# Moving low-part products to the end of ten weight tiles, one add to GpSimd, three exponentials behind the squares and one transpose a step up, in a hybrid decoder layer

## The chip, the core and the metric

The kernel runs on one core of a Trainium2 chip. The core has TensorE (PE: matrix products; its weight loads are listed as PEld), VectorE (DVE), ScalarE (ACT), GpSimd (POOL) and SyncE (SP); each takes its own instructions in order. ACT, SP and POOL also issue DMA transfers. The metric is the device time of one execution in microseconds (us), the median of three runs: 831.07 us before the change (829.67 to 834.61).

## What is computed

The reference is one layer on 512 tokens of 1024 channels, all in float32:

```
u = rmsnorm(h);  proj = u @ w_in      # GLU pairs, q, k, v, r, low-rank gate, gate A, gate B
c = a * sigmoid(g);  c = causal_depthwise_conv(c, width 31)
y_conv = silu(layernorm(c)) @ w_conv_out
gk = log_sigmoid(g_low @ w_gate_up + b_gate) / 16
o = chunked_gla(q, k, v, gk)          # 4 heads, chunks of 64 tokens
o = o * rsqrt(mean(o*o) + EPS) * gla_norm_g * silu(r)
y_gla = o @ w_gla_out
h = h + (sigmoid(gate_a) * y_conv + sigmoid(gate_b) * y_gla) @ w_o
u2 = rmsnorm(h);  z = causal_depthwise_conv(u2 @ w_ffn_up, width 3)
h = h + (silu(z_a) * z_b) @ w_ffn_down
return rmsnorm(h)
```

Inside a head the decays come from gk: b is the running sum of gk within a chunk of 64 tokens, and exp(b), exp(-b) and exp(b_last - b) scale q and k.

## The kernel before, in words

**Products in two parts.** Each float32 operand is split into a high part, rounded to the type fp32r, and a low part, the rest. A product is then three matmuls into one PSUM bank: low weight with high activation, high with low, and high with high. `mm3` issues these three (L395, L396, L397). A column tile (`col_tile`) holds 128 output channels over 512 tokens: eight k-steps of `mm3`, 24 matmuls, into one of five banks "mm". The result has channels on partitions. A second set of three banks is called "ax".

**Weights.** SP loads a tile of 128 x 1024 into `raw` (four buffers). `split_weight` makes `whi` (four buffers) by an ACT cast (L342; L323 for tiles that are handled in other ways). The low part `wlo` (four buffers) is made in one of two ways. Usually DVE subtracts (L351, L324). For tiles in the table `ADDED`, ACT writes the negated, rounded raw tile into `wlo` (L344), and POOL issues a DMA that adds the same weights from DRAM to it (L345), so that what remains is the rest; the low part is ready when that transfer has landed. A `wlo` buffer is written anew when the last matmul that reads it is through. `ADDED` holds, among others, five tiles of `w_glu` (4, 6, 8, 12 and 14), all eight of `w_qk`, and all of `w_gb` and `w_gla`.

**What sets the order.** The program is written in Python against a tile framework with a scheduler. It places each engine's instructions from the order in which the code stands, the data they need and the free buffers. Some stretches are pinned to the order written. `with tc.issue_after(x)` puts the instructions of the block that run on x's engine behind x there; other engines are not bound. The 31 convolution taps of each channel tile (L813, on DVE; the first one on ACT, L810) stand in lists, `chains`, from which a share is placed whenever a weight tile is taken, so DVE works at them beside the matmuls.

**The stages, by the times of the profile.** First normalisation and first v and r products (to about 32 us), GLU, r and v with the seven-product scheme for 2x2 blocks (to about 160), four heads (160 to 302), `w_gla`, `w_ga` and `w_conv` with the layer norm of the convolution (to about 435), `w_o` and the second norm (to about 490), then feed-forward.

**The heads.** The loop over h is staggered. In turn h it issues, for the new head h, `decays` (DVE: scan L1065, difference L1071, small copies L1075 to L1077; ACT: exponentials L1067, L1068, L1072), `queries` and `keys`; and for the old head h-1 `scores`, `states`, `outputs` and `gated`, with further weight tiles between them (`between`). `outputs` makes o in two pairs of token tiles: PE products (L1137, L1139), ACT squares with a running sum (L1142, twice for each pair), DVE adds EPS (L1144), POOL raises to the power -1/2 (`rsqrt`, L443), DVE multiplies by the root and the gate (L1150, twice for each pair). `gated` transposes o on PE (L1156), eight transposes of 128 x 128. Between the last matmul of `outputs` and these transposes PE has one weight tile to work at.

**The second norm.** `seven` runs `w_o` in steps. The token tiles of the residual are complete at different steps: tiles 0 and 1 after the step s4, tiles 2 and 3 after the last step, a22. A complete tile gets squares on ACT (L1336), the sum on DVE (L1341), the root on POOL (L443), the scaling into `un` on ACT (L491), transposes on PE (L474), the gain on DVE (L483) and the split into high part `uh` (ACT, L485) and low part `ul` (DVE, L486). `o_at` is called after the matmuls of each half step and places `to_channels`, the turn of a tile. The feed-forward begins with four tiles of `w_up`, each first for tokens 0 to 255 and then for 256 to 511, in matmuls of 256 columns.

Of the kernel before, what the change touches and what calls it, by code (L numbers as in the profile page):

```python
# [10 lines left out]
F32 = mybir.dt.float32  # L11
# [6 lines left out]
P = 128  # L18
# [27 lines left out]
UP_SEVEN = (6, 7, 10, 11, 14, 15, 18)  # L46
UP_BESIDE = (1, 3, 4, 5, 9, 20, 13, 16, 17)
ADDED |= {("w_up", j) for i in UP_BESIDE for j in (i, FT + i)}
SEVEN = {"w_o": KT // 2, "w_down": FT // 2, "w_r": KT // 2, "w_v": KT // 2}


# [27 lines left out]
def trunk_layer(ctx: ExitStack, tc: tile.TileContext, a: dict, out: bass.AP):  # L79
# [65 lines left out]
    gate_up = cp.tile([P, HEADS * DK], F32R, name="gate_up")  # L145
    ones = cp.tile([P, P], F32, name="ones")
    mhalf = cp.tile([P, NT], F32, name="mhalf")
    shares = cp.tile([P, P], F32, name="shares")
    run64 = cp.tile([P, T], BF16, name="run64")
    keep = cp.tile([P, P], U8, name="keep")  # L150
# [2 lines left out]
    def load_consts():  # L153
        tc.keep_in_program_order(nc.sync.dma_start(pp, a["pp"]))
        nc.gpsimd.memset(shares, -1.0 / D)
        nc.gpsimd.memset(run64, 1.0)
        nc.gpsimd.memset(run64[:, 0:T:64], 0.0)

        kf = tmp(P)
        nc.gpsimd.memset(kf, 1.0)  # L160
        nc.gpsimd.affine_select(
            kf, kf, pattern=[[1, P]], compare_op=ALU.is_ge, fill=0.0, base=0, channel_multiplier=-1
        )
        nc.gpsimd.tensor_copy(keep, kf)
        nc.gpsimd.memset(att, 0.0)
# [139 lines left out]
    def split_weight(between=None):  # L305
        if len(ready) < len(order):
            while len(raws) <= len(ready):
                load()
            raw = raws[len(ready)]
            name, spec = order[len(ready)]  # L310
            if name in SEVEN or name == "w_up7":
                raw = operand(name, raw, *spec) if name in SEVEN else up_operand(raw, *spec)
                n = raw.shape[-1]
                if name == "w_up7" and spec[1] == "m":
                    both = wp.tile([P, D], F32R, tag="raw", name=nm("wm"), bufs=4)
                    nc.scalar.copy(both[:, :T], raw)
                    nc.vector.tensor_tensor(both[:, T:], raw, both[:, :T].bitcast(F32), ALU.subtract)
                    ready.append((both[:, :T], both[:, T:]))
                    load()
                    return  # L320
                hi = wp.tile([P, D], F32R, tag="whi", name=nm("whi"), bufs=4)[:, :n]
                lo = wp.tile([P, D], F32R, tag="wlo", name=nm("wlo"), bufs=4)[:, :n]
                nc.scalar.copy(hi, raw)  # L323
                pace[0] = nc.vector.tensor_tensor(lo, raw, hi.bitcast(F32), ALU.subtract)  # L324
                if name in SEVEN:
                    sum_on(name, *spec)
                skipped = name in INNER and raws[len(ready)] is None
                ready.append((hi, lo))
                if not skipped:
                    load()  # L330
                return
            hi = wp.tile([P, D], F32R, tag="whi", name=nm("whi"), bufs=4)
            if order[len(ready)][0] == "w_low":
                nc.scalar.copy(hi, raw)
                if order[len(ready)][1] == 0:
                    part_lo = lambda t: t.rearrange("p (k c) -> p k c", c=P)[:, :, :RANK]
                    nc.vector.tensor_tensor(part_lo(hi), part_lo(raw), part_lo(hi.bitcast(F32)), ALU.subtract)
                ready.append((hi, None))
                load()
                return  # L340
            lo = wp.tile([P, D], F32R, tag="wlo", name=nm("wlo"), bufs=4)
            nc.scalar.copy(hi, raw)  # L342
            if order[len(ready)] in ADDED:
                pace[0] = nc.scalar.activation(lo, raw, AF.Copy, scale=-1.0)  # L344
                nc.gpsimd.dma_start(lo, a[name][spec], accum_op=ALU.add)  # L345
                ready.append((hi, lo))
                load()
                return
            if between:
                between()  # L350
            pace[0] = nc.vector.tensor_tensor(lo, raw, hi.bitcast(F32), ALU.subtract)  # L351
            ready.append((hi, lo))
            load()
# [37 lines left out]
    def mm3(acc, l, r, first, last, more=False):  # L391
# [4 lines left out]
        nc.tensor.matmul(acc, lh, rl, start=False, stop=False, **kw)  # L396
        nc.tensor.matmul(acc, lh, rh, start=False, stop=last, **kw)  # L397

    def col_tile(w, acts, acc=None, lo=0, hi=T):

        if acc is None:
            acc = mm_bank()
        for k in range(KT):
            s = slice(k * P, (k + 1) * P)
            ah, al = acts[k]
            mm3(acc[:, lo:hi], (w[0][:, s], w[1][:, s]), (ah[:, lo:hi], al[:, lo:hi]), k == 0, k == KT - 1)
        return acc

    def row_half(name, j0, n, acts, nk, done, tok_inner, middle=None):
# [641 lines left out]
    class Head:  # L1051
# [77 lines left out]
        def outputs(self):  # L1129
            self.o = tp.tile([P, NT, DV], F32, tag="x", name=nm("o"), bufs=3)  # L1130
            for g in range(2):
                po = ax_bank()
                ss = small(2, "ss2")
                for i in range(2):
                    p = 2 * g + i
                    half = po[:, i * DV : (i + 1) * DV]
                    nc.tensor.matmul(half, att[:, p, :], self.v(p), start=True, stop=p == 0)  # L1137
                    if p:
                        nc.tensor.matmul(half, flat(self.q, p, 0), self.s[p], start=False, stop=True)  # L1139
                for i in range(2):  # L1140
                    half = po[:, i * DV : (i + 1) * DV]
                    nc.scalar.activation(junk(DV), half, AF.Square, scale=1.0 / 16.0, accum_out=ss[:, i : i + 1])  # L1142
                v = small(2, "var2")
                nc.vector.tensor_scalar(v, ss, EPS, None, ALU.add)  # L1144
                r = rsqrt(v, 2)
                for i in range(2):
                    t = 2 * g + i
                    gate = sr[t, self.h // 2][:, (self.h % 2) * DV : (self.h % 2 + 1) * DV]
                    half = po[:, i * DV : (i + 1) * DV]
                    nc.vector.scalar_tensor_tensor(self.o[:, t, :], half, r[:, i : i + 1], gate, ALU.mult, ALU.mult)  # L1150
# [22 lines left out]
    def between(h, i):  # L1173
# [4 lines left out]
        else:  # L1178
            gate_b(6 + i)

    heads = [Head(h) for h in range(HEADS)]
    for h in range(HEADS + 1):
        old = heads[h - 1] if h else None
        new = heads[h] if h < HEADS else None
        if new:
            new.decays()
            if h == 0:
                for y in sr.values():
                    behind(lambda: nc.scalar.activation(y, y, AF.Silu))
# [167 lines left out]
    def o_at(step, i):  # L1357
        if (step, i) == ("n3", 0):
            u2.extend(new_acts())
            first = tp.tile([P, D], F32, tag="gain", name=nm("f2"), bufs=1)  # L1360
            to_channels(normed[0], u2, 0, lambda g: first[:, g * T : (g + 1) * T])
        if (step, i) == ("a22", 0):
            to_channels(normed[1], u2, 1, lambda g: btmp())

    seven("w_o", O_PAIRS, mixed, o_complete, o_at)
# [220 lines left out]
    def by_parts(w):  # L1586

        acc = mm_bank()
        for k in range(KT):
            s = slice(k * P, (k + 1) * P)  # L1590
            mm3(acc, (w[0][:, s], w[1][:, s]), acts2[k], k == 0, k == KT - 1)
            yield acc

    for gi, pairs in enumerate(GROUPS):
        acts = []
# [123 lines left out]
```

## Time and profile before

| what | value |
| --- | --- |
| median of three runs | 831.07 us (829.67 to 834.61) |
| the profiled execution, its own time | 828.47 us |
| its span, first to last instruction | 826.8 us |
| PE busy | 813.3 us, 98% of the span |
| DVE busy | 676.8 us, 82% |
| ACT busy | 471.0 us, 57% |
| POOL busy | 123.1 us, 15% |
| granted TensorE clock | 0.998 |

Busy time of PE is modelled: matmuls overlap, so that a matmul row of 0.39 us is followed by the next after about 0.23 us. What PE loses at a place is therefore read from the distances of the start times rather than from the idle column. A row of the timeline gives start, duration, engine, line, operation, what it writes and reads with shapes, a count, and in brackets the idle time ahead of it and what ended it. A small loss on PE is the time of the kernel; idle time of another engine is none.

### The profile page before, as it was taken

The numbers are of one execution on the slowest core, as the hardware profiler recorded it, in microseconds if no ns is written. First come the engines' busy times: TensorE is split into PE (matmuls) and PEld (weight loads), VectorE is DVE, ScalarE is ACT, GpSimd is POOL, SyncE is SP. The second block draws the span as 40 slices with busy tenths as digits, with TensorE's granted clock in tenths as the row PEclk, the third lists the DMA queues.
The fourth block names the chain that finished last, engine by engine and source line by source line (L and its number), as shares of the span: only waits on it lengthen the run. The fifth ranks groups of instructions, "written<-read, shape, count | busy, mean of one in ns | idle before, by whom it ended". The sixth has DMA issues, their size and how long they took to land.

```text
span 826.8 us, 11023 instructions
## 1 busy us (share of the span) xinstructions
PE 813.3 (98%) x4090; PEld 689.9 (83%) x4090; DVE 676.8 (82%) x991; ACT 471.0 (57%) x669; POOL 123.1 (15%) x144
## 2 busy tenths in 40 slices
PE   8999999999999999999999999999999999999996
PEld 7988878878888888888888898888788888988885
DVE  6898978999989889854689768789858888588896
ACT  7664546695443553359344659655446543667554
POOL 2021101311122121000001012111112111220111
PEclk9999999999999999999999999999999999999999
DMA  9999849558666578221447539356835647557562
GB/s 324 310 327 222 209 116 230 129 160 211 150 131 154 134 195 202 77 102 51 153 92 205 183 116 237 93 146 153 217 93 149 166 89 217 153 153 202 131 128 101
DMA packets 50213, 136.65 MB, mean 165 GB/s; under 512 B 4624, under 2 KB 17184, under 8 KB 50160
## 3 DMA queue, kind: packets, MB, share of 16 engines
q1 hardware_dynamic: 37456, 90.91, 31.2%
q0 software_dynamic: 12528, 44.83, 30.5%
q8 instruction: 32, 0.52, 0.3%
q10 hardware_dynamic: 176, 0.20, 0.1%
q14 instruction: 21, 0.17, 0.1%
HBM read 133.84 MB, written 6.29 MB: 169 GB/s over the span
## 4 chain that ended last, share of the span: by engine, by line
PE 78%; DVE 11%; DMA 4%; issue 3%; ACT 2%; POOL 1%; SPq 0%; POOLq 0%; ACTq 0%; DVEq 0%
PE mm L396 22%; PE mm L395 22%; PE mm L397 22%; DVE c L813 4%; PE ax L395 2%; DMA wlo<-in_w_glu_dram 2%; PE mm L663 2%; PE ax L396 2%; PE ax L397 2%; DVE wlo L324 1%; DMA kept<-rows 1%; DMA x<-in_x_dram 1%; PE ax L1137 1%; DVE tmp L1378 1%; PE ax L474 0%
## 5 line engine op out<-in xcount | busy, mean ns | idle before, releaser
L395 PE MATMUL mm<-uh,wlo 128*128 128x512 f32 (+1 forms) x636 | 237.5, 374 | 3.5 <-DMA wlo<-in_w_glu_dram 1.9
L396 PE MATMUL mm<-ul,whi 128*128 128x512 f32 (+1 forms) x636 | 234.9, 369 | 0.2 <-DVE ul L486 0.2
L397 PE MATMUL mm<-uh,whi 128*128 128x512 f32 (+1 forms) x636 | 234.5, 369 | 0.0
L813 DVE SCALAR_TENSOR_TENSOR c<-h,pp,c 128x507 f32<-128x507 f32 (+20 forms) x240 | 169.9, 733 | 2.8
L395 PEld LDWEIGHTS mm<-uh,wlo 128*128 128x128 f32 x636 | 119.9, 189 | 22.9 <-DMA wlo<-in_w_glu_dram 2.1
L397 PEld LDWEIGHTS mm<-uh,whi 128*128 128x128 f32 x636 | 119.8, 188 | 20.5
L396 PEld LDWEIGHTS mm<-ul,whi 128*128 128x128 f32 x636 | 120.1, 189 | 18.7 <-DVE ul L486 0.7
L342 ACT CAST whi<-raw 128x1024 fp32r<-128x1024 f32 x94 | 97.4, 1042 | 36.7 <-PE mm L397 29.0
L344 ACT ACTIVATE wlo<-raw 128x1024 fp32r<-128x1024 f32 x47 | 49.5, 1058 | 69.6 <-PE mm L395 65.5
L323 ACT CAST whi<-raw 128x1024 fp32r<-128x1024 f32 (+1 forms) x53 | 54.0, 1027 | 52.6 <-PE mm L397 36.1
L324 DVE TENSOR_TENSOR wlo<-raw,whi 128x1024 fp32r<-128x1024 f32 (+1 forms) x53 | 65.8, 1249 | 11.5 <-ACT whi L323 11.0
L1378 DVE SCALAR_TENSOR_TENSOR tmp<-mm,pp,tmp 128x511 f32<-128x511 f32 (+1 forms) x88 | 64.5, 742 | 12.6 <-ACT tmp L1376 12.2
L351 DVE TENSOR_TENSOR wlo<-raw,whi 128x1024 fp32r<-128x1024 f32 x47 | 56.9, 1220 | 16.7 <-ACT whi L342 16.3
L323 ACT CAST whi<-kept 128x1024 fp32r<-128x1024 f32 (+1 forms) x44 | 44.3, 1009 | 37.7 <-PE mm L397 25.6
L324 DVE TENSOR_TENSOR wlo<-kept,whi 128x1024 fp32r<-128x1024 f32 (+1 forms) x44 | 52.3, 1196 | 4.3 <-ACT whi L323 4.1
L1376 ACT ACTIVATE tmp<-mm,pp 128x512 f32<-128x512 f32 x44 | 33.3, 775 | 11.6 <-PE mm L397 11.6
L1298 DVE TENSOR_TENSOR hres<-hres,mm 128x512 f32<-128x512 f32 (+1 forms) x49 | 32.4, 670 | 2.5 <-PE mm L397 2.3
L345 POOL DMA_DIRECT2D wlo<-in_w_up_dram x18 | 15.6, 866 | 95.5 <-ACT wlo L344 77.6
L396 PE MATMUL mm<-wlo,sh 128*128 128x512 f32 x66 | 25.9, 393 | 0.0
L397 PE MATMUL mm<-whi,sh 128*128 128x512 f32 x66 | 25.7, 390 | 0.0
L395 PE MATMUL mm<-h,wlo 128*128 128x512 f32 x64 | 25.4, 397 | 0.0
L395 PE MATMUL mm<-whi,sl 128*128 128x512 f32 x66 | 25.2, 391 | 0.2 <-ACT whi L323 0.2
(361 smaller groups left out, 1635.1 us busy)
## 6 DMA issues: line engine op xcount, KB each, us to landing
raw<-in_w_up_dram SPq DMA_DIRECT2D x44, 512.0 KB, 4.4
wlo<-in_w_up_dram POOLq DMA_DIRECT2D x18, 512.0 KB, 7.4
raw<-in_w_glu_dram SPq DMA_DIRECT2D x16, 512.0 KB, 5.9
raw<-in_w_down_dram SPq DMA_DIRECT2D x15, 512.0 KB, 5.1
kept<-in_w_down_dram POOLq DMA_DIRECT2D x10, 512.0 KB, 5.3
raw<-in_w_v_dram SPq DMA_DIRECT2D x8, 512.0 KB, 6.0
rows<-in_w_r_dram SPq DMA_DIRECT2D x16, 256.0 KB, 6.4
raw<-in_w_qk_dram SPq DMA_DIRECT2D x8, 512.0 KB, 5.1
```

Of the source, the lines that this page charges most:

```text
L323: nc.scalar.copy(hi, raw)
L324: pace[0] = nc.vector.tensor_tensor(lo, raw, hi.bitcast(F32), ALU.subtract)
L342: nc.scalar.copy(hi, raw)
L344: pace[0] = nc.scalar.activation(lo, raw, AF.Copy, scale=-1.0)
L351: pace[0] = nc.vector.tensor_tensor(lo, raw, hi.bitcast(F32), ALU.subtract)
L395: nc.tensor.matmul(acc, ll, rh, start=first, stop=False, **kw)
L396: nc.tensor.matmul(acc, lh, rl, start=False, stop=False, **kw)
L397: nc.tensor.matmul(acc, lh, rh, start=False, stop=last, **kw)
L813: nc.vector.scalar_tensor_tensor(y[:, s:], c[:, : T - s], w, y[:, s:], ALU.mult, ALU.add)
L1298: nc.vector.tensor_tensor(hres[t, n][:, c], hres[t, n][:, c], x[:, c], op)
L1376: nc.scalar.activation(z, acc, AF.Identity, bias=pp[:, PP_FB + m : PP_FB + m + 1], scale=w[2])
L1378: nc.vector.scalar_tensor_tensor(z[:, s:], acc[:, : T - s], w[j], z[:, s:], ALU.mult, ALU.add)
```

## The change

Five edits. `LOW_LAST_IN` names ten tiles of `ADDED` (`w_glu` 4 and 8, all `w_qk`). In these, `col_products` issues the 16 products with the high weight first and the eight with the low weight last; all other column tiles keep their order, and the number of matmuls is the same everywhere. In `outputs` EPS is added on GpSimd from a small constant tile instead of on VectorE. From the third head on, the ACT instructions of `decays` stand behind the last square of the head two before it. The second norm's turn of token tile 1 is placed at the step ("n3", 1) instead of ("a22", 0). `by_parts` yields as before, after every third product.

```
-                ready.append((hi, lo))
+                ready.append((hi, lo, (name, spec) in LOW_LAST_IN))

+LOW_LAST_IN = {("w_glu", 4), ("w_glu", 8)} | {("w_qk", m) for m in range(KT)}

+    eps = cp.tile([P, 2], F32, name="eps")
+        nc.gpsimd.memset(eps, EPS)

+    def col_products(w, acts, acc, lo=0, hi=T):
+
+        late = [(1, 0, k) for k in range(KT)] if w[2:] and w[2] else []
+        todo = [p for k in range(KT) for p in ([(0, 0, k), (0, 1, k)] if late else [(1, 0, k), (0, 1, k), (0, 0, k)])]
+        todo += late
+        for n, (low_w, low_a, k) in enumerate(todo):
+            l, r = w[low_w][:, k * P : (k + 1) * P], acts[k][low_a][:, lo:hi]
+            nc.tensor.matmul(acc[:, lo:hi], l, r, start=n == 0, stop=n == len(todo) - 1)
+            yield n
+
     def col_tile(w, acts, acc=None, lo=0, hi=T):
-
         if acc is None:
             acc = mm_bank()
-        for k in range(KT):
-            s = slice(k * P, (k + 1) * P)
-            ah, al = acts[k]
-            mm3(acc[:, lo:hi], (w[0][:, s], w[1][:, s]), (ah[:, lo:hi], al[:, lo:hi]), k == 0, k == KT - 1)
+        for _ in col_products(w, acts, acc, lo, hi):
+            pass
         return acc

-                    nc.scalar.activation(junk(DV), half, AF.Square, scale=1.0 / 16.0, accum_out=ss[:, i : i + 1])
+                    squared[0] = nc.scalar.activation(junk(DV), half, AF.Square, scale=1.0 / 16.0, accum_out=ss[:, i : i + 1])
                 v = small(2, "var2")
-                nc.vector.tensor_scalar(v, ss, EPS, None, ALU.add)
+                nc.gpsimd.tensor_tensor(v, ss, eps, ALU.add)

+    squared = [None]
     heads = [Head(h) for h in range(HEADS)]
     for h in range(HEADS + 1):
         old = heads[h - 1] if h else None
         new = heads[h] if h < HEADS else None
+        if squared[0] is None:
+            new.decays()
+        elif new:
+            with tc.issue_after(squared[0].ins):
+                new.decays()
         if new:
-            new.decays()

-        if (step, i) == ("a22", 0):
+        if (step, i) == ("n3", 1):
             to_channels(normed[1], u2, 1, lambda g: btmp())
```

How the rows move on the engines is seen at three places. In the names, `uh` and `ul` are the high and low parts of the activations (two tiles each, for channels 0 to 511 and 512 to 1023), `whi` and `wlo` those of a weight tile, `mm` and `ax` PSUM banks; numbers are buffers' numbers and differ between the two programs, as do line numbers.

PE, the end of tile 8 of `w_glu`, before (the last k-step, then the next matmuls of the v products):

```order
L395 MATMUL mm_1121<-uh_107,wlo_1069 128x512
L396 MATMUL mm_1121<-ul_108,whi_1068 128x512
L397 MATMUL mm_1121<-uh_107,whi_1068 128x512
L395 MATMUL mm_979<-whi_1075,ul_108 128x512
L396 MATMUL mm_979<-wlo_1076,uh_107 128x512
```

And PE at the end of the same tile now:

```order
L409 MATMUL mm_1123<-uh_108,whi_1070 128x512
L409 MATMUL mm_1123<-ul_109,whi_1070 128x512
L409 MATMUL mm_1123<-uh_106,wlo_1071 128x512 x4
L409 MATMUL mm_1123<-uh_108,wlo_1071 128x512 x4
L398 MATMUL mm_981<-whi_1077,ul_109 128x512
```

The eight products with `wlo` stand together at the end, so the tile's first read of `wlo` comes after 16 matmuls, and its last read two matmuls later than before.

ACT, around the squares of head 0 (`junk,ss` rows), before; `tmp<-b` are exponentials of the decays of heads 2 and 3, `tmp<-tmp` the third one of head 2, `c<-h` the first tap of a convolution:

```order
L344 ACTIVATE wlo_1932<-raw_1707 128x1024
L342 CAST whi_1931<-raw_1707 128x1024
L1068 ACTIVATE tmp_1989<-b_1986 128x512
L1072 ACTIVATE tmp_1990<-tmp_1990 128x512
L344 ACTIVATE wlo_2002<-raw_1759 128x1024
L342 CAST whi_2001<-raw_1759 128x1024
L1142 ACTIVATE junk_1905,ss_345_1901<-ax_1900 128x256
L810 ACTIVATE c_2008<-h_1146,pp 128x512
L1142 ACTIVATE junk_1907,ss_345_1901<-ax_1900 128x256
L1067 ACTIVATE tmp_2241<-b_2239 128x512
L1142 ACTIVATE junk_1921,ss_351_1916<-ax_1915 128x256
L1142 ACTIVATE junk_1923,ss_351_1916<-ax_1915 128x256
```

And ACT at the same place now:

```order
L347 ACTIVATE wlo_1934<-raw_1709 128x1024
L347 ACTIVATE wlo_2004<-raw_1761 128x1024
L345 CAST whi_2003<-raw_1761 128x1024
L1152 ACTIVATE junk_1907,ss_345_1903<-ax_1902 128x256
L820 ACTIVATE c_2010<-h_1148,pp 128x512
L1152 ACTIVATE junk_1909,ss_345_1903<-ax_1902 128x256
L1152 ACTIVATE junk_1923,ss_351_1918<-ax_1917 128x256
L1152 ACTIVATE junk_1925,ss_351_1918<-ax_1917 128x256
L1077 ACTIVATE tmp_1990<-b_1988 128x512
L1078 ACTIVATE tmp_1991<-b_1988 128x512
L1082 ACTIVATE tmp_1992<-tmp_1992 128x512
```

All three exponentials of head 2 now follow the fourth square of head 0, and the first one of head 3 no longer stands among the squares. On DVE, the difference (L1071) and the small copies of head 2 and the scan (L1065) of head 3 move with them, from ahead of head 0's o (L1150) to behind it.

PE in the last steps of `w_o`, before (products of the step n3 read `sums`, those of a22 read `h`; `un` is the scaled token tile 1):

```order
L395 MATMUL mm_3801<-whi_4025,h_3771 128x512
L396 MATMUL mm_3801<-wlo_4026,h_3770 128x512
L397 MATMUL mm_3801<-whi_4025,h_3770 128x512
L474 MATMUL ax_4108<-ident,un_4016 128x128 x4
L474 MATMUL ax_4109<-ident,un_4016 128x128 x4
L395 MATMUL mm_3802<-whi_4019,h_3521 128x512
```

And PE there now:

```order
L398 MATMUL mm_3804<-whi_3971,sums_3778 128x512
L399 MATMUL mm_3804<-wlo_3972,sums_3778 128x512
L400 MATMUL mm_3804<-whi_3971,sums_3778 128x512
L484 MATMUL ax_4082<-ident,un_4018 128x128 x4
L484 MATMUL ax_4083<-ident,un_4018 128x128 x4
L398 MATMUL mm_3803<-whi_4021,h_3523 128x512
```

The eight transposes of tile 1 stand twelve matmuls earlier, ahead of the first half of a22. On DVE the gain and the split of tile 1 then stand ahead of the low parts of the first `w_up` tiles (L351), and the sum of tile 2 (L1341) behind the third of these instead of ahead of it; on ACT both squares of tiles 2 and 3 stand ahead of the scalings. SP's loads keep their order but for one `w_down` tile that is loaded behind two `w_up` tiles instead of ahead of them.

7 lines of the change are left out of this document (3 added, 4 removed).

## The prediction

> **What bounds the kernel now.** I read the page's busy times first, then PE's waits, then PE's start times at each wait, and last the other engines around them.
>
> ```profile
> PE 813.3 (98%) x4090; PEld 689.9 (83%) x4090; DVE 676.8 (82%) x991; ACT 471.0 (57%) x669; POOL 123.1 (15%) x144
> ```
>
> PE works for 813.3 of 826.8 us, and the rest includes the start and the end. The change adds and drops no matmul, so all it can save lies in PE's stalls. The list of PE's waits (us in all, times, longest) names three at which it aims:
>
> ```profile
> PE mm L395 <- DMA wlo<-in_w_glu_dram: 1.9, 2, 1.7
> PE mm L395 <- DMA wlo<-in_w_qk_dram: 1.6, 1, 1.6
> PE ax L1156 <- DVE o L1150: 0.2, 1, 0.2
> ```
>
> These columns are too small, since modelled ends cover part of a stall. The start times show the loss; a 512-column matmul is followed by the next after 0.23 us, a 256-column one after 0.12, where nothing waits:
>
> ```profile
> 60.32 0.39 PE L397 MATMUL mm<-uh,whi 128*128 128x512 f32 x1
> 60.90 0.47 PE L395 MATMUL mm<-uh,wlo 128*128 128x512 f32 x1 [0.19 <-DMA wlo<-in_w_glu_dram]
> 61.20 0.40 PE L396 MATMUL mm<-ul,whi 128*128 128x512 f32 x1
> ...
> 104.31 0.39 PE L397 MATMUL mm<-whi,f 128*128 128x512 f32 x1
> 106.38 0.50 PE L395 MATMUL mm<-uh,wlo 128*128 128x512 f32 x1 [1.69 <-DMA wlo<-in_w_glu_dram]
> 106.72 0.39 PE L396 MATMUL mm<-ul,whi 128*128 128x512 f32 x1
> ...
> 181.58 0.39 PE L397 MATMUL mm<-uh,whi 128*128 128x512 f32 x1
> 183.56 0.50 PE L395 MATMUL mm<-uh,wlo 128*128 128x512 f32 x1 [1.60 <-DMA wlo<-in_w_qk_dram]
> 183.90 0.39 PE L396 MATMUL mm<-ul,whi 128*128 128x512 f32 x1
> ...
> 212.11 0.38 PE L1156 MATMUL ax<-ident,o 128*128 128x128 f32 x2
> 212.66 1.15 PE L1156 MATMUL ax<-ident,o 128*128 128x128 f32 x6 [0.17 <-DVE o L1150]
> 213.57 0.47 PE L395 MATMUL mm<-uh,wlo 128*128 128x512 f32 x1
> ...
> 242.09 1.03 PE L1156 MATMUL ax<-ident,o 128*128 128x128 f32 x8
> 242.88 0.47 PE L395 MATMUL mm<-uh,wlo 128*128 128x512 f32 x1
> ...
> 474.86 0.28 PE L395 MATMUL mm<-uh,wlo 128*128 128x256 f32 x1
> 475.30 0.39 PE L396 MATMUL mm<-ul,whi 128*128 128x256 f32 x1 [0.16 <-DVE ul L486]
> 475.52 0.28 PE L397 MATMUL mm<-uh,whi 128*128 128x256 f32 x1
> ...
> 488.51 0.28 PE L395 MATMUL mm<-uh,wlo 128*128 128x256 f32 x1
> 488.78 0.39 PE L396 MATMUL mm<-ul,whi 128*128 128x256 f32 x1
> 489.01 0.28 PE L397 MATMUL mm<-uh,whi 128*128 128x256 f32 x1
> ```
>
> **The ten tiles with low products last.** Nothing is added: 24 matmuls and 24 weight loads before and after. The first read of `wlo` moves back by 16 matmuls, 16 x 0.23 = 3.7 us. Three stalls lie at such a first read. Tile 4 of `w_glu`: (60.90 - 60.32 - 0.23) + (61.20 - 60.90 - 0.23) = 0.42 us. Tile 8: (106.38 - 104.31 - 0.23) + (0.34 - 0.23) = 1.95 us. The second head's `w_qk`: (183.56 - 181.58 - 0.23) + (0.34 - 0.23) = 1.86 us. Together 4.23 us. PE also comes earlier to each by what was saved ahead of it. If no transfer moved with it, the third, 1.75 us late before, would be asked for 2.37 us earlier by the first two savings and 3.7 us later by the order, so 2.37 + 1.75 - 3.7 = 0.4 us of wait could be left. This transfer is started by ACT and POOL work that itself follows PE's earlier tiles, so I take all 4.23; the ends are 3.8 and 4.23.
>
> The price of the other side: the last read of `wlo` comes two matmuls (0.45 us) later, so the buffer is given to the fourth tile after it that much later, and ACT, in order, waits for it with what stands behind (weight casts, squares). The transfer after that takes
>
> ```profile
> DMA to landing us min/median/max: 5.2/7.2/11.9
> ```
>
> (`wlo` transfers between 40 and 215 us). From the write to the use lie three tiles of 24 x 0.23 = 5.4 us, 16 us, and even the longest transfer, with a write on ACT and an issue on POOL of about 1 us each ahead of it, needs 14; so a shift of 0.45 us is covered. Were it not, ten tiles would cost 4.5 us. I take 0, the near end, because PE waits at none of the later `wlo` tiles in the list.
>
> **EPS on GpSimd.** Eight DVE adds go; POOL gets eight. On DVE, one pair of head 0 looks like this, with POOL's two roots and the end of ACT's second square:
>
> ```profile
> 208.44 0.16 DVE L1144 TENSOR_SCALAR var<-ss 128x2 f32<-128x2 f32 x1
> 208.55 0.75 DVE L813 SCALAR_TENSOR_TENSOR c<-h,pp,c 128x510 f32<-128x510 f32 x1
> 209.92 0.87 DVE L1150 SCALAR_TENSOR_TENSOR o<-ax,rstd,h 128x256 f32<-128x256 f32 x2 [0.62 <-POOL rstd L443]
> ...
> 208.75 1.14 POOL L443 TENSOR_TENSOR rstd<-var,mhalf 128x2 f32<-128x2 f32 x1 [3.05 <-DVE var L1144]
> 211.01 1.07 POOL L443 TENSOR_TENSOR rstd<-var,mhalf 128x2 f32<-128x2 f32 x1 [1.13 <-DVE var L1144]
> ...
> 206.60 0.19 ACT L1142 ACTIVATION_READ_ACCUMULATOR junk<-ax 128x1 f32 x1
> ```
>
> The sum was there at 206.79, DVE came to the add only at 208.44, 1.65 us later, since taps stood ahead. PE would be at its transposes at 212.11 and lost there (213.57 - 212.11) - (242.88 - 242.09) = 0.67 us; the same eight transposes of head 1 show the undisturbed time. The fourth transpose needs all of o, at about 212.4. From 206.79 to there are 5.6 us, less 0.87 for the last two multiplications: 4.7 us for two adds and two roots on POOL. The trace has no add of 128x2 on POOL. Its nearest rows bound it:
>
> ```profile
> 808.05 0.19 POOL L1447 TENSOR_TENSOR var<-ss,var 128x1 f32<-128x1 f32 x1 [8.31 <-ACT junk L1432]
> 476.65 2.54 POOL L443 TENSOR_TENSOR rstd<-var,mhalf 128x1 f32<-128x1 f32 x1 [10.25 <-DVE var L1341]
> ```
>
> The first is an add near the kernel's end: 2 x 0.19 + 1.14 + 1.07 = 2.6 us, 2 us to spare. If each add is as slow as the roots beside the taps, 4 x 1.14 = 4.6, still in time. I take 0.19 to 1.14, where the nearest rows are, so the stall of 0.67 us goes. The second row is the upper end, and a rival below. POOL's next work behind the add is a `wlo` transfer, and it has the 16 us named above. The constant tile for EPS is one more small write on POOL at the start, beside the first loads.
>
> The Trainium skill, page "SBUF — State Buffer", section "Who interferes with whom", says that a DVE instruction with two SBUF inputs and a GpSimd instruction that reads SBUF exclude each other, and the later one fully blocks. The trace agrees: the root at 208.75 ends 0.59 us after the tap that began at 208.55 has ended. This rule speaks against the move, since taps fill DVE: by the free add the saving here is 0.67, by the rule with one tap for each step (4 x 1.14) it is 0.67 too, and with several taps for each it is a loss, the last rival below.
>
> **Exponentials behind the squares.** No instruction is added. On ACT one exponential leaves the squares of head 0 and three follow them; on DVE a difference, a scan and three small copies move behind o. Both lie beside PE's tile. Head 2's queries need the exponential when their tile, which begins at 213.57, ends 5.4 us later, at 219; the squares are through before the second root at 211.01, and the exponential follows at once. ACT then waits for the difference on DVE, with a `wlo` write and the casts of o behind it, whose cover is the same tile. Were it gone, each of heads 2 and 3 could lose up to the scan's 1.22 us; I take 0, as 8 us lie between. It serves the same 0.67 us, and is not counted twice.
>
> **The second norm.** PE's work is the same; eight transposes move ahead of twelve matmuls, 2.7 us. Their input was scaled at
>
> ```profile
> 466.43 1.34 ACT L491 ACTIVATE un<-hres,rstd 128x512 f32<-128x512 f32 x2 [1.44 <-POOL rstd L443]
> ```
>
> so is ready at 467.8, and the new place begins at about 468.5. The stall at 475.30, (0.44 - 0.12) + (0.22 - 0.12) = 0.42 us, should go, as gain and split begin 2.7 us earlier. What is late next is tile 2: its sum now waits for one more subtraction on DVE (about 1.2 us), but the root after it, which took the 2.54 us above, overlaps less of them. I take 0 there, between 0 and 0.4 us lost. Tile 3's squares no longer stand behind tile 2's scaling (1.34 us), so the stall at 488.78, (0.27 - 0.12) + (0.23 - 0.12) = 0.26 us, goes too. Together 0.68 us, between 0.3 and 0.68.
>
> On SP one load of `w_down` goes behind two of `w_up`:
>
> ```profile
> raw<-in_w_up_dram SPq DMA_DIRECT2D x44, 512.0 KB, 4.4
> ```
>
> It is used only after the group's `w_up` tiles, 5.4 us each. I take 0, at most 4.4 us.
>
> **The sum.** 4.23 + 0.67 + 0.68 = 5.58 us. The profiled execution took 828.47 us, 1.7 over its span, which gives 822.9. It is 2.6 us under the median of the runs shown, 831.07; from that, 825.5 us, 0.67% less. A change under 0.5% (4.2 us) is about what a measurement of this kernel can't tell from none.
>
> **Rivals.**
>
> *DVE holds PE.* From 138 to 209 us DVE has hardly a gap:
>
> ```profile
> 138.00:209.00 71.00, 69.40 (x317) 57.58 (x317) 69.45 (x108) 52.95 (x75) 12.65 (x13) 1.00 0.69 174
> ```
>
> (PE, PEld, DVE, ACT, POOL busy): 69.45 of 71 us. If DVE's work there does not begin earlier with PE, PE arrives 4.2 us sooner and waits at o. DVE comes to o earlier only by what moved behind it, a scan and a difference,
>
> ```profile
> 201.68 0.68 DVE L1071 TENSOR_TENSOR tmp<-b 128x512 f32<-128x512 f32 x1
> 203.31 1.22 DVE L1065 TENSOR_TENSOR_SCAN b<-run,h 128x512 f32<-128x512 bf16 x1
> ```
>
> and by small copies, about 2.1 us, to which 0.68 comes at the norm: 831.07 - 2.8 = 828.3. Against it: the stretch begins with work that follows PE's tiles, so it should shift.
>
> *The taps end late.* After the heads PE needs the finished taps at L870:
>
> ```profile
> 335.89 0.68 DVE L820 TENSOR_TENSOR btmp<-btmp,c 128x512 f32<-128x512 f32 x1
> 339.74 1.02 PE L870 MATMUL ax<-btmp,shares 128*128 128x512 f32 x2
> ```
>
> 3.2 us lie between. If DVE did not move at all, of the 4.9 us saved by then 1.7 would come back: 827.2. It belongs with the case before.
>
> *The waits only move.* If the transfers begin later by what PE gains, nothing is saved: 831. Against it: lateness is at most 1.95 us, cover 3.7.
>
> *GpSimd is locked out.* If each add takes 2.54 us, like the root of that length, two adds and two roots take 7.3 us, 2.6 more than the 4.7 there are. The three other heads have about the same, so four waits of 2.6 us come, 10.4: 831.07 - 5.58 + 10.4 = 835.9. The kernel is slower than before from the point where an add takes 1.95 us: (2 x 1.95 + 2.2 - 4.7) x 4 = 5.6. For it speaks DVE's tight row; against it, that DVE itself stops at o until the root is there, which lets GpSimd in.
>
> **How the numbers follow.** The forecast, 824 to 827: 0.57. DVE in part the bound, 827 to 830: 0.22. Waits only move, about 831: 0.08. GpSimd locked out, over 835.2: 0.09. Something unseen on the slow side: 0.04. Faster than 826.9: 0.57. Within 0.5%: 0.30. Slower: 0.13. The low end, 823.5, is the full sum from the fastest run shown (829.67 - 5.58 = 824.1) with a little for DVE's eight adds; the high end, 831.5, takes in the moved waits and leaves out the locked GpSimd.
>
> **What would show it.** Right: PE's list has no wait for `wlo` of `w_glu` or `w_qk`; 0.23 us between starts at the three places; eight transposes of head 0 in 0.8 us; adds on POOL of 0.2 to 1.1 us; no wait for `ul`. Wrong: waits for o in several heads, POOL adds over 1.95 us, waits at L870 or for `un`, or a new wait for `wlo` of another tile.

## The result, and the profile after

The changed kernel takes 827.30 us (median of 15 runs, 825.98 to 829.33), the kernel before 831.21 (15 runs, 829.29 to 836.14). The ratio is 0.9949, with a 95% interval of 0.9937 to 0.9961: 0.51% less, a small difference, but the whole interval lies under 1. The forecast was 825.5 us, with a range of 823.5 to 831.5.

The two profiled executions don't show this difference. The one after took 828.98 us, a long one of its kernel, the one before 828.47, a short one. So the profiles are compared place by place. PE's busy line, and the list of PE's waits, after:

```profile
PE 816.8 (99%) x4090; PEld 692.0 (84%) x4090; DVE 675.9 (82%) x983; ACT 471.4 (57%) x669; POOL 123.3 (15%) x153
```

```profile
PE ax L542 <- DVE ones L509: 1.1, 1, 1.1
PE ax L398 <- ACT mm L1581: 0.9, 1, 0.9
PE ax L484 <- DMA x<-in_x_dram: 0.5, 1, 0.5
PE ax L398 <- ACT mm L1587: 0.5, 1, 0.5
PE ax L484 <- ACT un L501: 0.4, 1, 0.4
PE mm L409 <- DMA wlo<-in_w_glu_dram: 0.2, 1, 0.2
```

The waits for `w_qk`, for o and for `ul` are gone. There is still one for a `wlo` of `w_glu`, one for `un` is new, and the wait for ACT at L1581 is longer than its counterpart before. Yet PE is busy 3.5 us more, with the same number of matmuls. PE's timeline after, at tile 6 of `w_glu`, at tile 8's first product with `wlo`, at head 0's transposes of o, at the second norm's tile 2, and at the first `n` product of the feed-forward:

```profile
72.38 0.39 PE L409 MATMUL mm<-uh,whi 128*128 128x512 f32 x1
73.00 0.50 PE L409 MATMUL mm<-uh,wlo 128*128 128x512 f32 x1 [0.23 <-DMA wlo<-in_w_glu_dram]
73.34 0.39 PE L409 MATMUL mm<-ul,whi 128*128 128x512 f32 x1
...
109.66 0.39 PE L409 MATMUL mm<-ul,whi 128*128 128x512 f32 x1
109.88 0.84 PE L409 MATMUL mm<-uh,wlo 128*128 128x512 f32 x3
...
210.23 0.39 PE L409 MATMUL mm<-uh,whi 128*128 128x512 f32 x1
210.46 1.03 PE L1166 MATMUL ax<-ident,o 128*128 128x128 f32 x8
211.25 0.48 PE L409 MATMUL mm<-uh,whi 128*128 128x512 f32 x1
...
479.52 0.28 PE L409 MATMUL mm<-uh,whi 128*128 128x256 f32 x1
480.19 1.27 PE L484 MATMUL ax<-ident,un 128*128 128x128 f32 x8 [0.40 <-ACT un L501]
481.22 0.36 PE L409 MATMUL mm<-uh,wlo 128*128 128x256 f32 x1
...
553.29 0.39 PE L398 MATMUL ax<-n,wlo 128*128 128x256 f32 x1 [0.91 <-ACT mm L1581]
```

Tile 8's `wlo` products follow 0.22 us behind the row ahead of them, and the eight transposes of o take 0.79 us: both stalls are gone. Tile 6 loses (0.62 - 0.23) + (0.34 - 0.23) = 0.50 us, and tile 2's transposes start 0.67 - 0.12 = 0.55 us late, with 0.12 more inside them.

What made PE busier is seen in the groups by line. Two kinds of product changed: those of `w_conv`, of which two in three read `ch` and one in three `c`, and those that read `f`, in the stage of r and v. Three of their groups stood like this before. The last number ahead of the idle column is the mean ns of one; it grows with the distance between starts (389 ns stand for 0.227 us from start to start, 397 for 0.235):

```profile
L395 PE MATMUL mm<-ch,wlo 128*128 128x512 f32 x64 | 24.9, 389 | 0.0
L396 PE MATMUL mm<-c,whi 128*128 128x512 f32 x64 | 24.9, 389 | 0.0
L395 PE MATMUL mm<-whi,f 128*128 128x512 f32 x48 | 18.7, 389 | 0.0
```

And after:

```profile
L409 PE MATMUL mm<-ch,wlo 128*128 128x512 f32 x64 | 25.4, 397 | 0.0
L409 PE MATMUL mm<-ch,whi 128*128 128x512 f32 x64 | 25.4, 397 | 0.0
L409 PE MATMUL mm<-c,whi 128*128 128x512 f32 x64 | 25.2, 393 | 0.0
L398 PE MATMUL mm<-whi,f 128*128 128x512 f32 x48 | 19.0, 395 | 0.0
L399 PE MATMUL mm<-wlo,f 128*128 128x512 f32 x48 | 19.0, 395 | 0.0
L400 PE MATMUL mm<-whi,f 128*128 128x512 f32 x48 | 18.9, 394 | 0.0
```

All six groups had 389 ns before. 64 x (8 + 8 + 4) + 48 x (6 + 6 + 5) ns is 2.1 us of PE's time that no wait shows. The windows table gives the same for `w_conv` and shows one more loss of this execution, at the start (PE busy and its matmuls first), before:

```profile
0.00:16.00 16.00, 13.61 (x68) 11.37 (x69) 10.20 (x17) 11.27 (x23) 3.08 (x15) 1.00 0.91 330
392.00:436.00 44.00, 44.00 (x196) 36.44 (x195) 32.90 (x51) 17.28 (x24) 1.82 (x3) 1.00 0.42 120
```

And after:

```profile
0.00:16.00 16.00, 14.39 (x62) 12.53 (x63) 9.44 (x16) 10.59 (x21) 3.12 (x16) 1.00 0.91 329
392.00:436.00 44.00, 44.00 (x190) 35.40 (x190) 31.57 (x50) 16.16 (x22) 2.64 (x3) 1.00 0.44 122
```

In 44 us PE, never idle, issues six matmuls fewer, 6 x 0.23 = 1.4 us. In the first 16 us it is six behind as well, 1.2 us by start times, though no product or transpose of this stretch is changed. The matmuls there are slower: the first eight transposes of x take 1.97 us, where they took 1.09 before. In a second profile of the kernel before (below) they take 1.97, too, so this much comes without the change. But the 60th matmul starts at 15.5 to 16.0 us in six of the eight profiles that have both the ten tiles and the add on GpSimd, and at 14.4 to 14.9 in the six others, so the change may have a part in the rest; these runs don't settle it.

Where do 32 bytes come in? The new tile `eps` has 8 bytes in each partition and takes a slot of 32. It stands behind `mhalf` among the constants, and the program's addresses show that every tile allocated behind it from that end of the memory (weights, activations, `h`, `c`) now begins 32 bytes further, at a multiple of 128 plus 32. Tiles allocated from the other end, `f` and `ch` among them, stay at multiples of 128. The slower products are those that read one tile that moved and one that didn't, and in the `w_conv` chain the `c` products between them.

### The profile page after: what moved, and what is told of

Read it like the earlier page. It is cut to its first block, busy times and chain, and to the rows that moved or that the text cites. A ratio compares the mean times of both kernels' runs of the same rounds, so it can differ in the third digit from the quotient of the medians.

```text
span 827.2 us, 11027 instructions
## 1 busy us (share of the span) xinstructions
PE 816.8 (99%) x4090; PEld 692.0 (84%) x4090; DVE 675.9 (82%) x983; ACT 471.4 (57%) x669; POOL 123.3 (15%) x153
## 4 chain that ended last, share of the span: by engine, by line
PE 86%; DMA 6%; DVE 4%; issue 2%; ACT 1%; POOL 1%; POOLq 0%; ACTq 0%; DVEq 0%; SPq 0%
PE mm L409 51%; PE mm L399 7%; PE mm L400 7%; PE mm L398 7%; PE mm L673 2%; PE ax L398 2%; PE ax L399 2%; PE ax L400 2%; DMA kept<-in_w_o_dram 2%; DMA wlo<-in_w_glu_dram 1%; DVE wlo L327 1%; PE ax L1147 1%; PE ax L484 1%; DMA kept<-rows 1%; DMA raw<-in_w_o_dram 1%
## 5 line engine op out<-in xcount | busy, mean ns | idle before, releaser
L409 PE MATMUL mm<-ul,whi 128*128 128x512 f32 (+1 forms) x608 | 226.8, 373 | 0.0
L409 PE MATMUL mm<-uh,whi 128*128 128x512 f32 (+1 forms) x608 | 226.5, 373 | 0.0
L409 PE MATMUL mm<-uh,wlo 128*128 128x512 f32 (+1 forms) x608 | 217.2, 377 | 0.3 <-DMA wlo<-in_w_glu_dram 0.2
L409 PEld LDWEIGHTS mm<-uh,whi 128*128 128x128 f32 x608 | 114.5, 188 | 20.3
L409 PEld LDWEIGHTS mm<-uh,wlo 128*128 128x128 f32 x608 | 114.7, 189 | 19.3 <-DMA wlo<-in_w_glu_dram 0.7
L409 PEld LDWEIGHTS mm<-ul,whi 128*128 128x128 f32 x608 | 114.7, 189 | 17.7
L409 PE MATMUL mm<-h,whi 128*128 128x512 f32 x128 | 39.5, 389 | 0.0
L409 PEld LDWEIGHTS mm<-h,whi 128*128 128x128 f32 x128 | 24.0, 188 | 5.2 <-issue 0.2
```

The lines of the kernel that those rows point to most:

```text
L409: nc.tensor.matmul(acc[:, lo:hi], l, r, start=n == 0, stop=n == len(todo) - 1)
```

## Experiments

Each time is a median, with the ratio to runs of the kernel before made beside it on the same chip (their medians were 831.1, 832.05 and 830.9 us). "EPS in mhalf" means the first edit below.

**The moved tiles.** Four kernels. In the first EPS lies in the slot of `mhalf`, so nothing moves:

```
-    mhalf = cp.tile([P, NT], F32, name="mhalf")
-    eps = cp.tile([P, 2], F32, name="eps")
+    halves = cp.tile([P, NT + 2], F32, name="mhalf")
+    mhalf, eps = halves[:, 0:NT], halves[:, NT : NT + 2]
```

> The changed kernel with EPS kept in two columns of the tile mhalf, whose 16 bytes a partition take a slot of 32, so that every other tile lies where it lay before the change. Theory (offset): the constant tile moved all tiles behind it by 32 bytes, and matmuls that read one operand from a tile that moved and one from a tile that did not (f in the row products, ch in w_conv) start 4 to 8 ns later each; without it those 335 matmuls are again 0.2267 us apart and the kernel takes about 2.2 us less than the changed one, 825.1 us. Rival (timing): the wider spacing comes from what the other engines do beside these tiles since the change; then nothing moves, 827.3 us.

825.0 us (823.04 to 827.68), ratio 0.9910 (0.9880 to 0.9941). The groups in its profile:

```profile
L409 PE MATMUL mm<-ch,wlo 128*128 128x512 f32 x64 | 24.9, 389 | 0.0
L400 PE MATMUL mm<-whi,f 128*128 128x512 f32 x48 | 18.7, 389 | 0.0
```

The second is the kernel before with the moved tiles alone:

```
     mhalf = cp.tile([P, NT], F32, name="mhalf")
+    gap = cp.tile([P, 2], F32, name="gap")
...
         nc.gpsimd.memset(shares, -1.0 / D)
+        nc.gpsimd.memset(gap, EPS)
```

> The kernel before with a constant tile of two columns behind mhalf that is written once and read by nobody; no other edit. Theory (offset): the 32 bytes alone make the products with f and ch slower, 335 x 4 to 8 ns = 2.2 us, so 833.4 us against 831.2, with 0.233 us between their starts. Rival (timing): no change, 831.2 us.

835.39 us (832.96 to 837.31), ratio 1.0033 (1.0015 to 1.0052), with the groups of the changed kernel:

```profile
L397 PE MATMUL mm<-ch,wlo 128*128 128x512 f32 x64 | 25.4, 397 | 0.0
L397 PE MATMUL mm<-whi,f 128*128 128x512 f32 x48 | 19.0, 395 | 0.0
```

So the 32 bytes alone widen the spacing, and undoing them alone takes it back. The rival on timing falls. The ratio is worth 2.7 us, the medians 4.3. More than the 2.1 of the groups is not explained by them: in this profile tile 8 of `w_glu` also waited 3.6 us for its `wlo`, with a halved clock behind it (below). Whether the moved tiles have to do with that stays open.

The third and fourth kernel keep `eps` and move the other end instead, by changing the unused space there:

```
-PADS = (384, 2016, 768)
+PADS = (384, 2112, 768)
```

> The changed kernel with 96 bytes more of unused space at the other end of the memory, so that f and ch, too, begin 32 bytes behind a multiple of 128, as the weights do. Theory (offset, of the two operands against each other): both are off by the same 32 bytes, so the 335 matmuls are 0.2267 us apart, 2.2 us less than the changed kernel, 825.1 us. Rival (offset of each operand for itself): nothing is mended, as more tiles are off now, 827.3 us or more.

826.83 us (826.10 to 827.13), ratio 0.9925 (0.9901 to 0.9949); and with 1984 in place of 2112:

> The changed kernel with 32 bytes less of unused space at the other end of the memory, so that f and ch move by the same 32 bytes as the weights and every distance between two tiles that a matmul reads is again that of the kernel before. Theory (distance between the two operands): with 96 bytes more, a distance of 128 bytes off the old one, products with ch fell from 0.234 to 0.230 us and those with f stayed at 0.233; with the old distance both are at 0.227 and the kernel takes 825.0 us. Rival (each tile's own start counts, and has to be a multiple of more than 32 bytes): still 0.233 us with f or ch, 827 us.

825.41 us (823.63 to 826.50), ratio 0.9921 (0.9899 to 0.9943). The groups with 2112:

```profile
L409 PE MATMUL mm<-ch,wlo 128*128 128x512 f32 x64 | 25.1, 393 | 0.0
L398 PE MATMUL mm<-whi,f 128*128 128x512 f32 x48 | 19.0, 396 | 0.0
```

And with 1984:

```profile
L409 PE MATMUL mm<-ch,wlo 128*128 128x512 f32 x64 | 24.9, 389 | 0.0
L398 PE MATMUL mm<-whi,f 128*128 128x512 f32 x48 | 18.7, 389 | 0.0
```

With 2112 both tiles of a product begin 32 bytes behind a multiple of 128, and the theory that this is enough fell: `f` is as slow as ever and `ch` half mended. With 1984 both also begin there, but at their old distance from each other, and all are at 389 again. So it is the distance between what lies at the two ends that counts, not where each tile begins, and 128 bytes off the old distance still cost something. The slower products are those that read one operand from each end, with the `c` products between them, so the two operands are the likely pair; but each run moves a whole end, and the pair is not shown apart from that. Which distances are good in general, and which part of the memory is in conflict, these runs don't say.

**The ten tiles alone** (the kernel before with `LOW_LAST_IN` and `col_products`, nothing else):

> The kernel before with the ten low-last tiles alone: EPS on VectorE as before and no new constant, the exponentials and the second norm as before. By the prediction's term 4.2 us go (0.42, 1.95 and 1.86), so 827.0 us. Rival (the waits move on): the wait for wlo of w_glu 6, 0.5 us in the changed kernel, and waits for o take part of it, 828.3 us. Rival (DVE holds PE): half of it comes back at o or at L870, 829 us.

829.34 us (827.06 to 831.18), ratio 0.9960 (0.9943 to 0.9977). The three stalls at the first `wlo` are gone; in the profiled execution the gain comes back at head 0's o. DVE's and PE's timeline there:

```profile
209.47 0.16 DVE L1152 TENSOR_SCALAR var<-ss 128x2 f32<-128x2 f32 x1
...
211.41 1.16 PE L1164 MATMUL ax<-ident,o 128*128 128x128 f32 x6 [1.47 <-DVE o L1158]
```

And the windows behind it, with the granted clock third from the end:

```profile
214.00:215.00 1.00, 1.00 (x4) 0.71 (x4) 1.00 (x2) 0.77 (x2) 0.00 (x0) 0.50 1.01 201
```

The second add of EPS on DVE began only at 209.47, behind the first o; its root, the second o and the transposes follow. By start times PE lost 2.5 us at the eight transposes (0.27 + 0.28 + 1.69 + 0.28), and from 213 to 216 us the granted clock was 0.50, with 0.43 us from matmul to matmul, 1.6 us more. This is the first rival of the prediction, DVE holding PE, in a form I had not priced: the clock comes on top. The profiled execution took 830.47 us, long for this kernel. Over all runs the ratio leaves 3.3 us of the gain (1.9 to 4.7; the medians differ by 1.8), so the full price at o is not paid in every execution.

**The heads' edits, and one of them.** First the heads' two edits without the tiles and the norm, EPS in mhalf:

> The kernel before with the edits of the heads alone: EPS added on GpSimd (its constant in two columns of mhalf, so that no tile moves) and the exponentials behind the squares; the order of the products and the second norm as before. By the prediction's term the stall of 0.67 us at head 0's transposes goes: 830.5 us. Theory (the parts need each other): the ten tiles alone took 1.8 us where 4.2 were summed, since PE then came earlier to o and waited 2.5 us there, with 1.6 us of halved clock behind it; here PE comes as late as before, so only 0.7 us goes, and the rest of what the whole saves without the moved tiles, 6.1 us, is seen only when both are made. Rival (the parts add up): 6.1 less 1.8 and less 0.7 for the norm leaves 3.6 us for this part alone, 827.5 us.

830.42 us (828.93 to 838.07), ratio 0.9984 (0.9965 to 1.0004): within what can't be told from none, as the theory said, and not the 3.6 us of the rival. In its profile head 0's transposes show no stall. Then the whole change with EPS in mhalf, and `new.decays()` back where it stood:

```
-        if squared[0] is None:
-            new.decays()
-        elif new:
-            with tc.issue_after(squared[0].ins):
-                new.decays()
         if new:
+            new.decays()
```

> The changed kernel with EPS in two columns of mhalf and the decays where they stood before, so that an exponential stands among the squares of head 0 and a scan and a difference ahead of its o on VectorE. Theory: PE, which comes 4 us earlier with the ten tiles, needs both edits of the heads; a wait for o of 0.5 to 2 us comes back at head 0, 826.0 us, more where the clock is halved behind it. Rival (GpSimd's add alone does it): 825.0 us, no wait for o.

824.60 us (823.47 to 825.74), ratio 0.9914 (0.9893 to 0.9935), no slower than with the exponentials behind. My theory that PE needs both edits fell. Head 0's transposes in its profile:

```profile
209.21 1.36 PE L1166 MATMUL ax<-ident,o 128*128 128x128 f32 x8
210.33 0.48 PE L409 MATMUL mm<-uh,whi 128*128 128x512 f32 x1
```

That is 1.12 us for the eight, 0.33 more than the undisturbed 0.79, where the ten tiles alone lost 2.5. The add on GpSimd does nearly all of it.

**The second norm's turn.** Alone:

> The kernel before with the second norm's turn of token tile 1 at the step n3, and nothing else. By the prediction's term 0.3 to 0.7 us go, 830.6 us, with no wait for ul. Rival (the wait moves): the transposes of tile 2 now wait for un, 0.55 us in the changed kernel, and nothing is gained, 831.2 us.

831.29 us (829.34 to 834.46), ratio 0.9997 (0.9981 to 1.0013). The wait for `ul` is gone from its list of waits, and none for `un` has come. And the whole change with EPS in mhalf without it:

> The changed kernel with EPS in two columns of mhalf (no tile moves) and the second norm's turn back at a22. By the prediction's term it is 0.3 to 0.7 us slower than with the turn at n3, 825.5 us against 825.0. Rival (the wait moves): the same, 825.0 us, and the wait of 0.7 us at the first n product of the feed-forward (ax from ACT's mm) is smaller, since it is the norm's move that delays ACT there.

826.18 us (825.49 to 827.58), ratio 0.9926 (0.9907 to 0.9944) against 0.9910 (0.9880 to 0.9941) with the turn. Both point at a gain, of 0.2 and 1.3 us by the ratios, and neither can tell it from none. PE's loss at the first `n` product was 0.9 us without the move and 1.2 with the move alone, so the move doesn't make it.

**The kernel before, once more**, for a second profile:

> The kernel before once more, for a second profile. Theory: the profiled execution was a short one (828.47 us, where the median is 831.1); in another the stalls for wlo of w_glu and w_qk are longer, and behind a stall of 1.7 us or more some 3 us follow at a granted clock of 0.50, which costs 1.6 us more. Rival: the same stalls as in the first profile, and the difference lies elsewhere.

832.44 us, one run. PE's timeline at its second head's `w_qk`:

```profile
182.84 0.39 PE L397 MATMUL mm<-uh,whi 128*128 128x512 f32 x1
185.30 0.50 PE L395 MATMUL mm<-uh,wlo 128*128 128x512 f32 x1 [2.07 <-DMA wlo<-in_w_qk_dram]
...
187.12 0.63 PE L397 MATMUL mm<-uh,whi 128*128 128x512 f32 x1
187.55 0.63 PE L395 MATMUL mm<-uh,wlo 128*128 128x512 f32 x1
```

And its windows there, one that ends where the clock falls and one that ends where it rises again (PE busy first, the granted clock third from the end):

```profile
182.47:185.88 3.41, 1.34 (x7) 0.80 (x6) 3.41 (x8) 3.04 (x4) 0.31 (x1) 1.00 0.98 228
185.88:189.30 3.41, 3.41 (x10) 2.64 (x9) 3.41 (x7) 1.87 (x3) 0.53 (x1) 0.50 1.07 284
```

What PE loses at each place, by start times, in us:

| place | before | before again | after |
| --- | --- | --- | --- |
| `w_glu` tile 4 | 0.42 | 0.41 | 0 |
| `w_glu` tile 6 | 0 | 0.63 | 0.50 |
| `w_glu` tile 8 | 1.95 | 2.04 | 0 |
| `w_qk`, second head | 1.86 | 2.34 | 0 |
| halved clock behind it | 0 | 1.57 | 0 |
| o of head 0 | 0.67 | 0 | 0 |
| second norm | 0.68 (`ul`) | 0.66 (`ul`) | 0.67 (`un`) |
| first `n` product | 0.21 | 1.44 | 1.17 |
| products with `f` and `ch` | 0 | 0 | 2.1 |

The theory holds for `w_qk` and its clock, but not for its 1.7 us: tile 8's stall of 2.0 us in the same profile cost no clock. The wait at the first `n` product belongs to both kernels and comes and goes, so the 1.0 us that the pair of profiles seemed to lose there by the change can't be put down to it. Tile 6's wait, too, stands in profiles of both.

**Further tiles.** Tile 6 low-last as well, EPS in mhalf:

> The changed kernel with EPS in two columns of mhalf, and with tile 6 of w_glu low-last, too. A wait for its wlo stood in the profiles of the changed kernel (0.4 us), of that with 96 bytes more (0.5) and of the second look at the kernel before (0.5), and in none of the kernel with EPS in mhalf. Theory: where it comes it goes, 0 to 0.5 us, 824.7 us. Rival (held longer): the buffer that tile 6 holds 0.45 us longer delays tile 12 or 14, same or up to 0.5 us slower, 825.3 us.

824.82 us (823.51 to 826.86), ratio 0.9920 (0.9897 to 0.9942): the same as without. And all tiles of `ADDED`:

> The changed kernel with EPS in two columns of mhalf, and with the low products last in every column tile whose low part is made by a transfer (w_gb, w_gla, the other w_glu and those w_up tiles, beside the ten). Theory (holding wlo 0.45 us longer costs nothing): 825.0 us, and no new wait for wlo. Rival (the price is real): each later wlo comes up to 0.45 us later, and PE waits at several of some twenty w_gb, w_gla and w_up tiles, 2 to 8 us, 827 to 833 us.

826.70 us (825.67 to 827.69), ratio 0.9941 (0.9918 to 0.9964), some 0.2 to 0.3% over the two versions measured beside it (824.82 and 824.60 us), with intervals that overlap. No wait for a `wlo` appears; two for DVE do:

```profile
302.12 0.50 PE L409 MATMUL mm<-h,whi 128*128 128x512 f32 x1 [0.52 <-DVE h L1170]
...
571.00 0.50 PE L398 MATMUL mm<-whi,yl 128*128 128x512 f32 x1 [1.70 <-DVE yl L1407]
```

So the order may have a price where no stall pays for it, though not the one that the rival named; whether it is one, and how it reaches DVE, isn't settled.

The three shortest versions (825.0, 824.82 and 824.60 us), all without moved tiles, can't be told apart. Each is about 2.5 us under the changed kernel.

## Why the prediction was right or wrong

*The ten tiles, 4.23 us: right in mechanism, and the cover held.* All three stalls go, and no later tile shows a wait that is shown to come from holding `wlo` (tile 6's stands in the second profile of the kernel before, too). The size was read from a short execution. In that second profile the same places cost 4.79 us and 1.57 of halved clock behind them. The sum had no term for a clock that falls behind a stall.

*EPS on GpSimd, 0.67 us: right for what was seen, too small for what it does.* The stall itself comes and goes: it is 0.67 us in the first profile of the kernel before and absent in the second, where PE came later. With the tiles alone PE lost 2.5 us at o and 1.6 in clock; with the heads' edits added, and the norm as before, the ratio goes from 0.9960 to 0.9926, 2.8 us (0.7 to 4.9 by the two intervals). The term was made on the old arrival of PE, although the same text had PE come 4 us earlier. The add, its duration as least, median and greatest ns, after:

```profile
L1154 POOL TENSOR_TENSOR var<-ss,eps x8: 184/212/594, 205.2 to 294.2; 128x2 f32<-128x2 f32 x8
```

All eight lie between 0.18 and 0.59 us, inside the range taken (0.19 to 1.14) and far from the 1.95 at which the last rival decides. Head 0's adds and roots on POOL, with a DVE tap beside them:

```profile
205.23 0.39 POOL L1154 TENSOR_TENSOR var<-ss,eps 128x2 f32<-128x2 f32 x1 [1.19 <-ACT junk L1152]
205.70 0.72 POOL L453 TENSOR_TENSOR rstd<-var,mhalf 128x2 f32<-128x2 f32 x1
206.40 0.49 POOL L1154 TENSOR_TENSOR var<-ss,eps 128x2 f32<-128x2 f32 x1
...
206.09 0.74 DVE L823 SCALAR_TENSOR_TENSOR c<-h,pp,c 128x511 f32<-128x511 f32 x1
```

The second add ends at 206.89, 0.06 us behind the tap. The Trainium skill, page "SBUF — State Buffer", section "Who interferes with whom", has a DVE instruction with two SBUF inputs and a GpSimd read of SBUF exclude each other; this row agrees, and the price here is the rest of one tap, not several. All eight adds fit: the four that began while such a DVE instruction ran (0.23 to 0.59 us) end 0.05 to 0.06 us behind it, and the four others take 0.18 to 0.20.

*Exponentials behind the squares: counted with the 0.67, and needed for little of it.* Without this edit 0.33 us stays at o, and the time is the same.

*The second norm, 0.68 us: the stalls go, the gain in time is not shown.* The stalls for `ul` are gone in all eight profiles with the move. What the text named as late next, tile 2, came in the profiled execution and took 0.67 us, over the 0 to 0.4 given; it came in one more of the eight (the version without the exponentials' edit) and not in that of the move alone. The ratio of the move alone, 0.9997 (0.9981 to 1.0013), holds both 0.68 and nothing.

*The constant tile, "one more small write on POOL": the step that failed.* Its write costs nothing that is seen, but its place does. It moves every tile behind it by 32 bytes, 336 products become 4 to 8 ns slower, and 2.1 us go that no list of waits names. The sum of 5.58 us less these 2.1 is 3.5, inside what the ratio gives, 3.2 to 5.2. Without the moved tiles the time is 825.0 us, where the forecast was 825.5; with them 827.3. That 825.0 and 825.5 meet so closely is partly chance, since the clock's 1.6 us was not in the sum and the norm's 0.7 is not shown.

*Rivals.* DVE as the bound holds for the ten tiles alone, and the add on GpSimd removes it. The result, 827.3, lies just outside the 824 to 827 of the forecast's own case and in the 827 to 830 of this rival, for a reason that is neither's: the moved tiles. That the wide range of 823.5 to 831.5 holds it says little. Two things that the text named as signs of being wrong did come, the wait for `un` and one for the `wlo` of another tile, 6; neither accounts for the 2.3 us between 825.0 and 827.3. No new loss came at the taps of L870, GpSimd was not locked out, and the waits did not only move.

## What to carry to other kernels

A new tile, however small, moves whatever is allocated behind it: look at the addresses before and after, keep the distance between the two operands of a matmul, and put a few new constants into slack that is there. A loss without a wait is found by the mean duration of the same group in both profiles. One profiled execution can be short by several microseconds (828.47 where the median was 831.2), so take stalls from two of them, and price a stall at a new arrival time together with the clock behind it.

## What the runs showed of the hardware

The distance in memory between the tiles that a matmul reads changes the spacing of 512-column matmuls in fp32r. As means of the start distances it is 0.227 us at the old distances, 0.233 to 0.235 with one operand 32 bytes off (0.231 for the `c` products between them), and 0.228 to 0.233 at 128 bytes off. Both operands moved by the same 32 bytes run at full rate.

A stall can cost more than itself. Behind stalls of 2.2 us (the second profile of the kernel before), 2.5 us in pieces (the ten tiles alone) and 3.6 us (the moved tiles alone) the granted clock was 0.50 for 3.4 us, and the next eight or so matmuls came every 0.43 us, about 1.6 us lost. Behind stalls of 1.6 to 1.9 us it stayed at 1.00, and behind one of 2.3 us (tile 8 with the heads' edits alone) too. The traces' records of the clock point to a reason. Each of the three stretches at 0.50 lasts 3.41 us, and the stretches at 1.00 ahead of them last 52, 61 and 30 times as long, so these changes fit a grid of 3.41 us. In the step ahead of each drop PE stood idle, by start times, for 2.3 to 2.6 us. In no other step of the fourteen profiles, their first 12 and last 15 us left out, was it more than 1.9. The stall of 2.3 us that cost no clock, from 105.15 to 107.48 us, is cut in two by its grid at 106.65, 1.5 us before and 0.8 behind:

```profile
103.24:106.65 3.41, 2.08 (x10) 1.38 (x8) 3.41 (x6) 2.10 (x2) 0.00 (x0) 1.00 0.91 238
106.65:110.07 3.41, 2.58 (x11) 2.16 (x12) 3.41 (x6) 0.00 (x0) 0.00 (x0) 1.00 0.01 4
```

The Trainium skill, page "TensorE: Matmul & The Clock Gate", section "HAM oscillation — how this bites in real kernels", warns of PE gaps above about 3.4 us. Here a gap of 2.2 us was enough in one execution, so the measurement decides. The Trainium skill, same page, section "What's actually happening", has the clock judged over a window that runs freely, by which one gap could count and a like one not. The grid in these traces agrees.

The root on POOL (128x2) takes 0.69 to 0.72 us in five of the eight cases after, where no DVE instruction with two SBUF inputs was running as it began. Where one was (the three others, and all eight before) it takes 1.03 to 1.20 us and ends 0.54 to 0.59 us behind that instruction.
